# One product of block 0's second matmul gets a second level, and W2's operand sums move along the schedule

## The chip, the cores and the metric

The kernel runs on one core of a Trainium2 chip. Times are device microseconds (us) of one launch; a version's time is the median of its runs. A ratio is the mean time of one kernel's fast runs over the mean of the other's fast runs of the same rounds, so it is not quite the ratio of the medians quoted beside it. Engines are called PE (TensorE), DVE (VectorE), ACT (ScalarE), POOL (GpSimd) and SP (SyncE, which here only issues transfers). In the lines of the profile, `arena` is the kernel's on-chip memory, bX, bY, bZ and bW are the banks that PE's products go to, and `w1s` and `w2s` hold parts and sums of W1 and W2 in device memory. L432 is line 432 of the kernel; the numbers shift by some lines from version to version. The granted clock is PE's clock as a share of full speed.

## The reference

```python
# x (16, 512, 768), w1 (768, 3072), b1 (3072), w2 (3072, 768), all float32
y = np.matmul(x, w1) + b1
y = 0.5 * y * (1.0 + erf(y / np.sqrt(2.0)))
return np.matmul(y, w2)
```

## The kernel before

The 8192 rows of x form eight blocks of 1024. Both matrix products use the scheme that multiplies two matrices, each cut into 2 x 2 parts, with seven products of half size in place of eight; the price is sums of parts before ("operand sums") and after. In blocks 2 to 7 the second matmul (by W2) uses the scheme twice: each of its seven products is again seven. Blocks 0 and 1 are different, because there the operand sums of W2 have still to be made and stored for the later blocks.

- Block 0's second matmul is four **row units** (`Unit2`), each seven products of 12 matmuls of 384 columns.
- Block 1's has three products (1, 4, 2) done with a second level, one **two-level unit** each (`UnitH`, 7 x 12 matmuls of 192 columns), and then four **lean** row units with the four other products.

The order is: row units of block 0, two-level units, lean units, block 2. While PE works on a unit, "fill" functions put other work into six slots of it, in program order: DVE sums, and transfers on the SP queue. A W2 sum is popped from the list `slow`; its store to memory is put on SP one slot later, by `drain`.

```python
        def split_w2(p, t=None, q=None):                  # four operand sums of W2 for product p
            ...
            for n, a, b in ((7, b22, b12), (5, b12, b11), (6, b22, t[5]), (4, b21, t[6])):
                def f(n=n, a=a, b=b):
                    tt(t[n], a, b, SUB)                    # DVE
                    puts.append(lambda: put(n, t[n]))      # SP: stored when drain() comes next
                later(WB, f, slow if q is None else q)
            ...

        def fill_lean(sb, k, slot):                        # lean unit k of block 1
            U = NU + k
            drain(slot)
            ...                                            # row sums
            if k == 0 and slot == 6:
                for t in range(3):
                    transpose_dma(2, t)                    # x of block 2, tiles 0 to 2: SP
                load_next_x(2, range(3, 6))                # tiles 3 to 5: POOL, into the same 3 buffers
            if k == 1 and slot == 2:
                for n in range(2):
                    load_wt(2 * NH + n)                    # two W1 tiles for block 2: SP
            if k == 1 and slot == 4:
                for t in range(3, 6):
                    transpose_dma(2, t)
                load_next_x(2, range(6, 8))
            if k == 2 and slot == 4:
                for t in range(6, 8):
                    transpose_dma(2, t)
            if k == 3 and slot == 4:
                x_sums(2, soon)                            # DVE; PE wants the first at block 2's start
            ...                                            # two more W1 tiles (k == 3, slot 5)
```

So x of block 2 goes through three buffers: load, transpose, load into the freed buffer, transpose, and once more. I call this the **x chain**.

Of the kernel before, what the change touches and what calls it, by code (L numbers as in the profile page):

```python
# [22 lines left out]
def kernel(  # L23
# [129 lines left out]
    o_stage = o_wt + 2 * WT_N  # L153
# [7 lines left out]
    for slot, off in ((T2, o_x0), (T1, o_x0 + W2_N + 2 * GS_N), (T4, o_x1 + XT_N)):  # L161
        w2v[slot] = cut(off, W2_N, "p (h c n) -> p h c n", h=2, c=NH)
    GS = [cut(o, GS_N, "p (c r) -> p c r", c=NH)
          for o in (o_x0 + W2_N, o_x0 + W2_N + GS_N, o_x1, o_x1 + GS_N)]
    osbs = [cut(o, PAR).bitcast(FP32).rearrange("p (a n) -> p a n", a=2)
            for o in (o_wt, o_x1 + 2 * GS_N)]
    par1, par4 = [cut(o, PAR).bitcast(FP32).rearrange("p (r t h n) -> p r t h n", r=2, t=2, h=2)
                  for o in (o_wt, o_x1 + 2 * GS_N)]
    par11 = cut(o_w2, W2P).bitcast(FP32).rearrange("p (c n) -> p c n", c=NH)[:, 0:8, 0:N4].rearrange(
        "p (r t h) n -> p r t h n", r=2, t=2)  # L170
    osbs1 = [cut(XT_N + k * PAR, PAR).bitcast(FP32).rearrange("p (a n) -> p a n", a=2)
             for k in range(2)]

    def lev_strip(c, r):
        return [Gs[0][k // 2][:, c:c + NQ, k % 2, r:r + 2 * P] for k in range(4)]
# [10 lines left out]
    with tc.manual_schedule():  # L186
# [58 lines left out]
        staged = [0]  # L245
# [6 lines left out]
        def split_w2(p, t=None, q=None):  # L252

            b11, b12, b21, b22 = quarters(p)

            def put(q, src):
                nc.sync.dma_start(out=w2s[p, q][:], in_=src)

            if t is None:
                t = {n: stage[(staged[0] + k) % len(stage)] for k, n in enumerate((7, 5, 6, 4))}  # L260
                staged[0] += 4
            for n, a, b in ((7, b22, b12), (5, b12, b11), (6, b22, t[5]), (4, b21, t[6])):
                def f(n=n, a=a, b=b):
                    tt(t[n], a, b, SUB)
                    puts.append(lambda: put(n, t[n]))
                later(WB, f, slow if q is None else q)
            return t
# [73 lines left out]

        def half_sums(c, ks=(0, 1, 2)):
# [16 lines left out]
        def lev_sums(i, c0=0, c1=NQ, ks=(0, 1, 2, 3), q=None, p=None, levs=None):  # L359

            A = OPERAND[ORDER[i] if p is None else p]
# [50 lines left out]
        class Unit2:  # L412
# [9 lines left out]
            def mm(self, p, dst, first, c0, c1):  # L422
                if self.lean and p in (1, 2, 4):
                    return
# [3 lines left out]
                for c in range(c0, c1):  # L428
                    a = {1: G1[:, c, 0, r], 2: G2[:, c, 0, r], 4: G2[:, c, 1, r],
# [12 lines left out]
            def c12(self):  # L442
                return self.o[:, 0, N2:N]

            def c22(self):
                return self.o[:, 1, N2:N]

            def right_done(self):
                c0 = N2 if self.lean else 0
                nc.sync.dma_start(out=orr[:, self.sb * 8 + self.u, c0:N], in_=self.o[:, 0, c0:N])  # L450

            def left_done(self, row, bank):
                if self.lean and row == 0:
                    return
                if self.lean:
                    tt(self.o[:, 1, 0:N2], bank[:, 0:N2], self.rows(par4), ADD)
                else:
                    nc.scalar.copy(out=self.o[:, row, 0:N2], in_=bank[:, 0:N2])
                if row == 1:
                    nc.sync.dma_start(out=orr[:, self.sb * 8 + NU + self.u, :],  # L460
                                      in_=self.o[:, 1, :])
# [98 lines left out]
        class UnitH(Unit3):  # L560

            def __init__(self, g, sb, m):
                self.g, self.sb, self.p = g, sb, HYBRID[m]
# [3 lines left out]
                self.add = par1 if self.p == 2 else None  # L567
                self.dst = {1: par1, 4: par4, 2: par11}[self.p]
                self.alloc = lambda: None

            def mm(self, q, dst, first, c0, c1):
                A, s = OPERAND[self.p], self.lev
# [18 lines left out]

        HYBRID = (1, 4, 2)
        hyb_lev = [lev_strip(0, 0), lev_strip(NQ, 0), lev_strip(0, 2 * P)]
        hyb_w = {}

        def wb_at(off):
            return cut(off, WB, "p (c n) -> p c n", c=NQ)
# [52 lines left out]
        def p6(u):  # L650
            u.mm(6, bY[u.g % 2], False, 0, u.C)
            on_act = isinstance(u, Unit3) or (isinstance(u, Unit2) and u.lean) or (isinstance(u, Unit1) and u.sb >= ONE and u.g % 2)
# [287 lines left out]
        def fill_mm2_one(sb, U, slot):  # L940
            if slot == 1:
# [5 lines left out]
                if U == 0:  # L947
                    for p in (1, 2, 3, 5, 6, 7, 4):
                        raw_w2(p)
                    for p in (5, 6, 7, 3):  # L950
                        split_w2(p)
                    hyb_w[1] = split_w2(1)
# [8 lines left out]
            if slot == 4 and U + 1 < NU:  # L961
                g_sum(1, U + 1, q=soon)
            if U + 1 == NU and slot == 2:
                lev_sums(None, p=HYBRID[0], levs=hyb_lev[0])
# [10 lines left out]
        def fill_hyb(sb, m, slot):  # L975
            drain(slot)
            if m == 0 and slot == 1:
                o = (o_x0 + W2_N, o_x0 + W2_N + WB, o_wt + PAR, o_wt + PAR + WB)
                hyb_w[4] = split_w2(4, dict(zip((5, 6, 7, 4), map(wb_at, o))), queue)
                lev_sums(None, p=HYBRID[1], levs=hyb_lev[1])  # L980
            if m == 1 and slot == 1:
                lev_sums(None, p=HYBRID[2], levs=hyb_lev[2])
                o = (o_x1, o_x1 + WB)
                hyb_w[2] = split_w2(2, dict(zip((5, 6, 7, 4), [wb_at(k) for k in o] +
                                                [stage[staged[0] % len(stage)], hyb_w[1][7]])), queue)
            if m == 2 and slot == 2:
# [4 lines left out]
            if slot == 6:  # L991
                flush(queue)
                if m == 2:
                    load_next_x(2, range(3))

        def fill_lean(sb, k, slot):
# [10 lines left out]
            if slot == 4 and k + 1 < NU:  # L1007
                g_sum(1, U + 1, q=soon)
            if slot > 1:
                sums(1200)  # L1010
            if k == 0 and slot == 6:
# [18 lines left out]
            if slot == 6 and k == NU - 1:  # L1030
                flush(soon)
                flush(queue)
                drain(slot)
# [95 lines left out]
```

## Time and profile before

| | before |
|---|---|
| median, range | 852.62 us, 852.40 to 853.05 (6 runs) |
| span of the profiled run | 850.6 us |
| granted clock | 1.0 |
| block 0's row units to the end of the lean units, first to last 384-column matmul start | 109.76 us |
| matmul spacing, 384 and 192 columns | 162.5 and 82.5 ns |

The prediction shows the lines that carry the bound (start, length, queue, line, operation, output<-input, count): PE's pieces follow each other without a gap. Two more lines will be needed, from the timelines of SP and POOL of the kernel before (start, length, queue, line, operation, output<-input, count): the two W1 tiles, and load 6 of x.

```profile
200.23 1.01 SPq L219 DMA_DIRECT2D arena<-w1s  x2
214.10 0.54 POOL L299 DMA_DIRECT2D arena<-in_x_dram  x1 [8.65 <-DMA arena<-arena]
```

The W1 tiles are issued 3.5 us ahead of x loads 3 to 5, and have landed (205.86 and 209.13) before those land (210.2 to 212.2). In brackets is POOL's idle time and what ended it: load 6 waited for a transpose, `arena<-arena`, to free its buffer.

### The profile page before, as it was taken

What the parts mean: (1) busy time and instruction counts of PE and PEld (TensorE: products, weight loads), DVE (VectorE), ACT (ScalarE), POOL (GpSimd) and SP (SyncE); (2) the same over time, 40 slices, a digit from 0 to 9 for tenths busy, and PEclk for the clock granted to TensorE, in tenths of its full rate; (3) what the DMA queues carried; (4) which work ended last, traced back from release to release, by engine and by line L of the source; (5) the groups of instructions that cost most, each with busy time, mean ns of one, the idle gap of its engine ahead of it and who ended that gap; (6) DMA issues with size and microseconds to landing.
All of it is one profiled execution on the core that took longest, in us unless ns stands there. A gap on an engine that the chain in (4) does not pass through costs nothing.

```text
span 850.6 us, 16487 instructions
## 1 busy us (share of the span) xinstructions
PE 845.5 (99%) x6432; PEld 569.6 (67%) x6432; DVE 667.2 (78%) x1126; ACT 421.3 (50%) x686; POOL 84.1 (10%) x135
## 2 busy tenths in 40 slices
PE   9999999999999999999999999999999999999998
PEld 5444446687544897449964499645995469944798
DVE  5766678786657998679976799768996699956998
ACT  4777761122277513773148822487216771267611
POOL 5021100002100002000020000210002100010000
PEclk9999999999999999999999999999999999999999
DMA  9998777659999699987999689995999949984398
GB/s 229 199 284 170 165 160 277 234 195 218 234 331 207 194 332 372 296 177 236 332 381 266 155 291 335 361 293 111 315 351 344 283 111 328 356 311 172 101 310 283
DMA packets 143522, 219.05 MB, mean 258 GB/s; under 512 B 61756, under 2 KB 84724, under 8 KB 143444
## 3 DMA queue, kind: packets, MB, share of 16 engines
q1 hardware_dynamic: 117824, 179.74, 67.3%
q0 software_dynamic: 25440, 38.15, 20.6%
q8 instruction: 50, 0.82, 0.4%
q14 instruction: 28, 0.23, 0.1%
q10 hardware_dynamic: 180, 0.11, 0.0%
HBM read 180.30 MB, written 47.87 MB: 268 GB/s over the span
## 4 chain that ended last, share of the span: by engine, by line
PE 95%; DMA 4%; DVE 0%; ACT 0%; issue 0%; POOL 0%; DVEq 0%; ACTq 0%
PE bY L388 21%; PE bY L493 15%; PE bX L388 14%; PE bX L493 10%; PE bZ L388 7%; PE bW L388 7%; PE bZ L493 5%; PE bW L493 5%; PE bY L432 5%; DMA arena<-in_x_dram 2%; PE bZ L432 2%; PE bW L432 2%; PE bX L432 2%; DMA arena<-in_w_dram 1%; PE bY L580 1%; PE bX L580 1%
## 5 line engine op out<-in xcount | busy, mean ns | idle before, releaser
L191 DVE TENSOR_TENSOR arena<-arena 128x768 f16<-128x768 f16 (+4 forms) x630 | 403.4, 671 | 7.5 <-PE bW L432 1.1
L388 PEld LDWEIGHTS <-arena 128*128 128x128 f16 x1974 | 192.6, 98 | 224.0 <-issue 0.4
L493 PEld LDWEIGHTS <-arena 128*128 128x128 f16 x3528 | 292.1, 98 | 8.4 <-issue 0.4
L388 PE MATMUL bY<-arena 128*128 128x512 f16 x846 | 214.4, 379 | 0.1
L613 DVE TENSOR_TENSOR arena<-bY,arena 128x512 f32<-128x512 f32 (+1 forms) x102 | 69.4, 681 | 127.0 <-PE bY L388 90.3
L493 PE MATMUL bY<-arena 128*128 128x192 f16 x1500 | 138.3, 246 | 0.0
L388 PE MATMUL bX<-arena 128*128 128x512 f16 x564 | 138.2, 379 | 0.0
L606 ACT COPY bY<-bX 128x512 f32<-128x512 f32 (+1 forms) x143 | 78.6, 550 | 119.4 <-DVE arena L542 82.0
L404 ACT ACTIVATE arena<-arena,b1t 128x1024 f16<-128x1024 f32 x94 | 108.0, 1149 | 54.0 <-DVE arena L641 54.0
L626 ACT COPY arena<-bW 128x512 f32<-128x512 f32 (+1 forms) x147 | 81.1, 552 | 90.7 <-PE bW L493 43.9
L493 PE MATMUL bX<-arena 128*128 128x192 f16 x1020 | 93.1, 246 | 0.1
L641 DVE TENSOR_TENSOR arena<-bZ,arena 128x512 f32<-128x512 f32 (+1 forms) x102 | 69.3, 679 | 22.2 <-PE bZ L388 18.2
L388 PE MATMUL bW<-arena 128*128 128x512 f16 x282 | 76.2, 379 | 0.0
L388 PE MATMUL bZ<-arena 128*128 128x512 f16 x282 | 76.2, 379 | 0.0
L432 PEld LDWEIGHTS <-arena 128*128 128x128 f16 x528 | 51.6, 98 | 34.1 <-issue 0.2
L525 POOL DMA_DIRECT2D out_dram<-arena x42 | 30.6, 729 | 406.4 <-DVE arena L637 370.2
L409 ACT ACTIVATE arena<-bX,b1t 128x512 f16<-128x512 f32 x94 | 64.0, 681 | 10.0 <-PE bX L388 10.0
L409 ACT ACTIVATE arena<-bY,b1t 128x512 f16<-128x512 f32 x94 | 63.4, 674 | 0.0
L657 ACT COPY bZ<-bY 128x512 f32<-128x512 f32 (+1 forms) x54 | 29.0, 537 | 65.7 <-DVE arena L641 31.4
L299 POOL DMA_DIRECT2D arena<-in_x_dram x60 | 32.7, 550 | 248.2 <-DMA arena<-arena 137.9
L493 PE MATMUL bW<-arena 128*128 128x192 f16 x504 | 48.4, 246 | 0.0
L493 PE MATMUL bZ<-arena 128*128 128x192 f16 x504 | 48.4, 246 | 0.0
(60 smaller groups left out, 401.8 us busy)
## 6 DMA issues: line engine op xcount, KB each, us to landing
arena<-w2s SPq DMA_DIRECT2D x294, 288.0 KB, 4.7
arena<-w1s SPq DMA_DIRECT2D x72, 672.0 KB, 7.0
out_dram<-arena POOLq DMA_DIRECT2D x42, 384.0 KB, 7.2
w2s<-arena SPq DMA_DIRECT2D x49, 288.0 KB, 3.8
arena<-in_x_dram POOLq DMA_DIRECT2D x60, 192.0 KB, 7.1
w1s<-arena SPq DMA_DIRECT2D x12, 672.0 KB, 6.1
arena<-in_w_dram POOLq DMA_DIRECT2D x17, 384.0 KB, 7.6
out_dram<-arena SPq DMA_DIRECT2D x17, 384.0 KB, 3.4
```

What stands on the lines that cost most here:

```text
L191: nc.vector.tensor_tensor(out=o, in0=a, in1=b, op=op)
L299: nc.gpsimd.dma_start(out=xhs[t], in_=xr[:, sb * 8 + t, :])
L388: nc.tensor.matmul(out=dst[:, 0:RH], lhsT=w1_op(self.wt, slot)[:, c, :], rhs=a[:, c, :], start=first and c == 0, stop=c == self.C - 1, ski ...
L404: nc.scalar.activation(out=self.G[1][:, hi, :, :], in_=self.tmp, func=GELU, bias=b1t[:, 2 * hi + 1:2 * hi + 2])
L409: nc.scalar.activation(out=self.G[0][:, hi, row, :], in_=bank[:, 0:RH], func=GELU, bias=b1t[:, 2 * hi:2 * hi + 1])
L432: nc.tensor.matmul(out=dst[:, 0:N2], lhsT=a, rhs=w[:, :, c, :], start=first and c == 0, stop=c == self.C - 1, skip_group_check=True)
L493: nc.tensor.matmul(out=dst[:, t * N4:(t + 1) * N4], lhsT=a, rhs=w[:, c, :], start=first and c == 0 and t == ts[0], stop=c == NQ - 1, skip_ ...
L525: eng.dma_start(out=orr[:, s0:s0 + 2, right * N2:(right + 1) * N2], in_=self.dst[:, r].rearrange("p t h n -> p t (h n)"))
L606: nc.scalar.copy(out=bY[u.g % 2][:, 0:u.F], in_=bX[u.g % 2][:, 0:u.F])
L613: nc.vector.tensor_tensor(out=u.c22(), in0=bY[u.g % 2][:, 0:u.F], in1=w[:, 0:u.F], op=ADD)
L626: nc.scalar.copy(out=w[:, 0:u.F], in_=bW[:, 0:u.F])
L641: nc.vector.tensor_tensor(out=u.c12(), in0=bZ[:, 0:u.F], in1=w[:, 0:u.F], op=ADD)
```

## The change

Its intent: product 2 of block 0 leaves the four row units and becomes a fourth two-level unit, seven eighths of the columns. Its operands need DVE time and buffers in block 0's units, so only W2 products 6, 1, 4 and 2 are summed there; 7 and 5 move into the two-level units and 3 into the lean units. The core of the diff (buffer addresses and names cut):

```diff
             def mm(self, p, dst, first, c0, c1):          # Unit2
-                if self.lean and p in (1, 2, 4):
+                if p == 2 or self.lean and p in (1, 4):
                     return
...
-        HYBRID = (1, 4, 2)
+        HYBRID = ((0, 2), (1, 1), (1, 4), (1, 2))
...
         def fill_mm2_one(sb, U, slot):                    # block 0's row units
-                    for p in (5, 6, 7, 3):
-                        split_w2(p)
-                    hyb_w[1] = split_w2(1)
+                    for p, t in ((6, (0, 1, 2, 3)), (1, (4, 5, 0, 1)), (4, (2, 3, 4, 5)), (2, (0, 1, 2, 5))):
+                        split_w2(p, t)
...
         def fill_hyb(sb, m, slot):                        # two-level units
+            if m == 1 and slot == 6:
+                split_w2(7, (6, 7, 6, 7))
+                split_w2(5, (6, 7, 6, 7))
+            if slow and (m == 1 or slot in (1, 4, 6)):
+                slow.pop(0)[1]()
...
         def fill_lean(sb, k, slot):
+            if k == 0 and slot == 4:
+                split_w2(3, (1, 2, 3, 4))
             if slot > 1:
                 sums(1200)
+            if slow and slot in (2, 5):
+                slow.pop(0)[1]()
```

Also new: six stored W2 quarters of products 1 and 4 are read back (`load_w2s`), copies of one bank go from DVE to ACT, and the output buffers are laid out anew.

More of the change, by code (lines that the diff above doesn't have):

```diff
@@ L152 @@
     tmps1 = [tmp_at(o_tmp + 4 * k * RH) for k in range(2)]
-    o_stage = o_wt + 2 * WT_N
+    o_stage = o_wt + 2 * N + PAR
     stage = [cut(o_stage + k * WB, WB, "p (c n) -> p c n", c=NQ)
@@ L164, with strip, wb_at @@
           for o in (o_x0 + W2_N, o_x0 + W2_N + GS_N, o_x1, o_x1 + GS_N)]
-    osbs = [cut(o, PAR).bitcast(FP32).rearrange("p (a n) -> p a n", a=2)
-            for o in (o_wt, o_x1 + 2 * GS_N)]
-    par1, par4 = [cut(o, PAR).bitcast(FP32).rearrange("p (r t h n) -> p r t h n", r=2, t=2, h=2)
-                  for o in (o_wt, o_x1 + 2 * GS_N)]
+    osbs = [[cut(o, n).bitcast(FP32) for o, n in zip(oo, (2 * N2, 2 * N))]
+            for oo in ((o_x1 + 2 * GS_N + 2 * N + 2 * N2, o_wt),
+                       (o_x1 + 2 * GS_N + 2 * N, o_x1 + 2 * GS_N))]
+    assert 2 * N + 4 * N2 <= PAR
+    par02, par1, par4 = [cut(o, PAR).bitcast(FP32).rearrange(
+        "p (r t h n) -> p r t h n", r=2, t=2, h=2) for o in (o_wt + 2 * N, 2 * XT_N, o_x1 + 2 * GS_N)]
     par11 = cut(o_w2, W2P).bitcast(FP32).rearrange("p (c n) -> p c n", c=NH)[:, 0:8, 0:N4].rearrange(
         "p (r t h) n -> p r t h n", r=2, t=2)
-    osbs1 = [cut(XT_N + k * PAR, PAR).bitcast(FP32).rearrange("p (a n) -> p a n", a=2)
-             for k in range(2)]
-    def lev_strip(c, r):
-        return [Gs[0][k // 2][:, c:c + NQ, k % 2, r:r + 2 * P] for k in range(4)]
+    osbs1 = [[cut(XT_N + k * PAR, 2 * N2).bitcast(FP32),
+              cut(XT_N + k * PAR + 2 * N2, 2 * N).bitcast(FP32)] for k in range(2)]
+    def strip(h, a, c, r):
+        return Gs[0][h][:, c:c + NQ, a, r:r + 2 * P]
+    def wb_at(off):
+        return cut(off, WB, "p (c n) -> p c n", c=NQ)
+    hyb_lev = [[strip(0, 0, 0, 0), strip(1, 1, 0, 0), Gs[0][1][:, 0:NQ, 0, 2 * P:RH], strip(1, 1, NQ, 0)],
+               [strip(0, 1, 0, 0), strip(0, 0, NQ, 0), strip(0, 1, NQ, 0), strip(0, 0, 0, 2 * P)],
+               [strip(0, 1, 0, 2 * P), strip(0, 0, NQ, 2 * P), strip(0, 1, NQ, 2 * P),
+                strip(1, 1, NQ, 2 * P)],
+               [strip(0, 0, 0, 0), strip(0, 1, 0, 0), strip(0, 0, NQ, 0), strip(0, 1, NQ, 0)]]
+    spare = stage + [wb_at(2 * XT_N + PAR + k * WB) for k in range(2)]
+    hyb_w = {2: {7: stage[0], 5: stage[1], 6: stage[2], 4: stage[5]},
+             1: dict(zip((7, 4, 5, 6), map(wb_at, (o_x0 + W2_N, o_x0 + W2_N + WB, o_x1, o_x1 + WB)))),
+             4: {7: wb_at(o_x1), 4: wb_at(o_x1 + WB), 5: stage[3], 6: stage[4]}}
     b1t = wp.tile([P, 2 * NH], FP32, name="b1t")
@@ L244 @@
         SLOT = {1: B11, 2: B21, 3: B22, 4: T4, 5: T1, 6: T2, 7: T3}
-        staged = [0]
         puts, raws = [], []
@@ L250, in quarters, with split_w2 @@
             return w[:, 0, 0:NQ, :], w[:, 1, 0:NQ, :], w[:, 0, NQ:NH, :], w[:, 1, NQ:NH, :]
-        def split_w2(p, t=None, q=None):
+        def split_w2(p, t, q=None):
             b11, b12, b21, b22 = quarters(p)
@@ L257, in put @@
                 nc.sync.dma_start(out=w2s[p, q][:], in_=src)
-            if t is None:
-                t = {n: stage[(staged[0] + k) % len(stage)] for k, n in enumerate((7, 5, 6, 4))}
-                staged[0] += 4
+            t = {n: spare[k] for n, k in zip((7, 5, 6, 4), t)}
             for n, a, b in ((7, b22, b12), (5, b12, b11), (6, b22, t[5]), (4, b21, t[6])):
@@ L266, in split_w2, with load_w2s @@
                 later(WB, f, slow if q is None else q)
-            return t
+        def load_w2s(p, qs):
+            for q in qs:
+                nc.sync.dma_start(out=hyb_w[p][q], in_=w2s[p, q][:])
         def raw_w2(p):
@@ L340, with operand @@
                    5: GA, 6: GB, 7: G1[:, :, 1, :]}
+        HYBRID = ((0, 2), (1, 1), (1, 4), (1, 2))
+        def operand(sb, p):
+            return OPERAND[p] if sb else Gs[0][1][:, :, 0, :]
         def half_sums(c, ks=(0, 1, 2)):
@@ L357, in lev_of, with lev_sums @@
             return lev[(i - 1) % 2] if i else lev0
-        def lev_sums(i, c0=0, c1=NQ, ks=(0, 1, 2, 3), q=None, p=None, levs=None):
-            A = OPERAND[ORDER[i] if p is None else p]
+        def lev_sums(i, c0=0, c1=NQ, ks=(0, 1, 2, 3), q=None, m=None):
+            A = OPERAND[ORDER[i]] if m is None else operand(*HYBRID[m])
+            levs = None if m is None else hyb_lev[m]
             a11, a12 = A[:, c0:c1, 0:2 * P], A[:, NQ + c0:NQ + c1, 0:2 * P]
@@ L428, in mm @@
                 for c in range(c0, c1):
-                    a = {1: G1[:, c, 0, r], 2: G2[:, c, 0, r], 4: G2[:, c, 1, r],
+                    a = {1: G1[:, c, 0, r], 4: G2[:, c, 1, r],
                          3: GS[3][:, c, :], 5: GS[0][:, c, :], 6: GS[1][:, c, :],
@@ L442, in c12 @@
             def c12(self):
-                return self.o[:, 0, N2:N]
+                return self.o[0]
             def c22(self):
-                return self.o[:, 1, N2:N]
+                return self.o[1][:, N2:N]
             def right_done(self):
-                c0 = N2 if self.lean else 0
-                nc.sync.dma_start(out=orr[:, self.sb * 8 + self.u, c0:N], in_=self.o[:, 0, c0:N])
+                nc.sync.dma_start(out=orr[:, self.sb * 8 + self.u, N2:N], in_=self.o[0])
             def left_done(self, row, bank):
-                if self.lean and row == 0:
+                if row == 0:
+                    if not self.lean:
+                        nc.scalar.copy(out=self.rows(par02), in_=bank[:, 0:N2])
                     return
                 if self.lean:
-                    tt(self.o[:, 1, 0:N2], bank[:, 0:N2], self.rows(par4), ADD)
+                    tt(self.o[1][:, 0:N2], bank[:, 0:N2], self.rows(par4), ADD)
                 else:
-                    nc.scalar.copy(out=self.o[:, row, 0:N2], in_=bank[:, 0:N2])
-                if row == 1:
-                    nc.sync.dma_start(out=orr[:, self.sb * 8 + NU + self.u, :],
-                                      in_=self.o[:, 1, :])
+                    nc.scalar.copy(out=self.o[1][:, 0:N2], in_=bank[:, 0:N2])
+                nc.sync.dma_start(out=orr[:, self.sb * 8 + NU + self.u, :], in_=self.o[1])
         units3 = {}
@@ L562, in __init__ @@
             def __init__(self, g, sb, m):
-                self.g, self.sb, self.p = g, sb, HYBRID[m]
+                self.g, (self.sb, self.p) = g, HYBRID[m]
                 self.lev, self.w = hyb_lev[m], dict(hyb_w[self.p])
@@ L566, in __init__ @@
                 self.w.update({1: b11, 2: b21, 3: b22})
-                self.add = par1 if self.p == 2 else None
-                self.dst = {1: par1, 4: par4, 2: par11}[self.p]
+                self.add = {0: par02, 1: par1}[self.sb] if self.p == 2 else None
+                self.dst = {1: par1, 4: par4, 2: par11}[self.p] if self.sb else par02
                 self.alloc = lambda: None
             def mm(self, q, dst, first, c0, c1):
-                A, s = OPERAND[self.p], self.lev
+                A, s = operand(self.sb, self.p), self.lev
                 for c in range(NQ):
@@ L590, in finish @@
                             in_=self.dst[:, n // 2, n % 2])
-        HYBRID = (1, 4, 2)
-        hyb_lev = [lev_strip(0, 0), lev_strip(NQ, 0), lev_strip(0, 2 * P)]
-        hyb_w = {}
-        def wb_at(off):
-            return cut(off, WB, "p (c n) -> p c n", c=NQ)
         def p1(u, c0, c1):
@@ L651, in p6 @@
             u.mm(6, bY[u.g % 2], False, 0, u.C)
-            on_act = isinstance(u, Unit3) or (isinstance(u, Unit2) and u.lean) or (isinstance(u, Unit1) and u.sb >= ONE and u.g % 2)
+            on_act = isinstance(u, Unit3) or isinstance(u, Unit2) or (isinstance(u, Unit1) and u.sb >= ONE and u.g % 2)
             if isinstance(u, Unit3) and u.add is not None:
@@ L962, in fill_mm2_one @@
                 g_sum(1, U + 1, q=soon)
+            if U + 2 == NU and slot == 5:
+                lev_sums(None, m=0, ks=(0, 1, 3))
+            if U + 1 == NU and slot == 4:
+                lev_sums(None, m=0, ks=(2,))
             if U + 1 == NU and slot == 2:
-                lev_sums(None, p=HYBRID[0], levs=hyb_lev[0])
+                lev_sums(None, m=1, ks=(0, 1, 2))
             if slot > 1:
@@ L977, in fill_hyb @@
             if m == 0 and slot == 1:
-                o = (o_x0 + W2_N, o_x0 + W2_N + WB, o_wt + PAR, o_wt + PAR + WB)
-                hyb_w[4] = split_w2(4, dict(zip((5, 6, 7, 4), map(wb_at, o))), queue)
-                lev_sums(None, p=HYBRID[1], levs=hyb_lev[1])
-            if m == 1 and slot == 1:
-                lev_sums(None, p=HYBRID[2], levs=hyb_lev[2])
-                o = (o_x1, o_x1 + WB)
-                hyb_w[2] = split_w2(2, dict(zip((5, 6, 7, 4), [wb_at(k) for k in o] +
-                                                [stage[staged[0] % len(stage)], hyb_w[1][7]])), queue)
-            if m == 2 and slot == 2:
+                load_w2s(1, (7, 4))
+                lev_sums(None, m=1, ks=(3,))
+            if m == 0 and slot == 4:
+                load_w2s(1, (5, 6))
+            if m == 0 and slot == 5:
+                lev_sums(None, m=2)
+            if m == 1 and slot == 5:
+                lev_sums(None, m=3, ks=(0, 1, 2))
+            if m == 1 and slot == 6:
[3 more added lines that the diff above has]
+                slow.pop(0)[1]()
+            if m == 2 and slot == 1:
+                load_w2s(4, (7, 4))
+                lev_sums(None, m=3, ks=(3,))
+            if m == 3 and slot == 2:
                 for k in (0, 1):
@@ L992, in fill_hyb @@
                 flush(queue)
-                if m == 2:
+                if m == 3:
                     load_next_x(2, range(3))
@@ L1032, in fill_lean @@
                 flush(queue)
+                flush(slow)
                 drain(slot)
```

## The prediction

> **What bounds the kernel now.** I read the page first, then the chain of work in order of time for 116 to 236 us (the stretch that the change touches), then the engines one by one there. The page's busy line and the shares of the chain:
>
> ```profile
> PE 845.5 (99%) x6432; PEld 569.6 (67%) x6432; DVE 667.2 (78%) x1126; ACT 421.3 (50%) x686; POOL 84.1 (10%) x135
> PE 95%; DMA 4%; DVE 0%; ACT 0%; issue 0%; POOL 0%; DVEq 0%; ACTq 0%
> ```
>
> TensorE (PE) is busy 99% and is 95% of the chain; the 4% of DMA is the head, before the first product. Busy matmul time alone can hide gaps, so I looked at the spacing of pieces in the chain, at the hand-over from block 0's units (L432, 384 columns) to the two-level units (L580, 192 columns) and back:
>
> ```profile
> 168.91 1.95 PE bX L432 x12
> 170.86 0.99 PE bX L580 x12
> 171.85 1.95 PE bY L432 x12
> ...
> 193.54 0.99 PE bX L580 x12
> 194.53 1.02 PE bY L580 x12
> 195.56 1.95 PE bW L432 x12
> ```
>
> Each piece starts where the last ended (168.91 + 1.95 = 170.86). Twelve matmuls of 384 columns take 1.95 us, 162.5 ns each; twelve of 192 take 0.99, 82.5 ns each. The only irregular pieces between 119 and 236 us are one of 1.02 (0.03 too long) and one of 2.01 (0.06 too long). Taking every matmul's start to the next start, the excess over these paces sums to some 4.5 us in the whole kernel, 3.6 of it in the first 40 us. So **PE's columns set the time**, and no wait is left to remove in the changed stretch: it can gain only what it takes off PE, and lose whatever stall it makes.
>
> **What the Trainium skill says.** "TensorE: Matmul & The Clock Gate", section "Wait — 56ns, not 53.3ns?": warm start-to-start is columns / 2.4 GHz plus about 2.5 ns. That is 162.5 and 82.5 ns for 384 and 192; the trace agrees to the digit, and granted clock is 1.00 in every 10 us stretch after the head. So splitting a matmul in two costs only 2.5 ns. "Perfetto Trace Analysis", "Identifying the Most-Contended Engine": matmul busy share is no measure of headroom, look at weight loads; PEld is at 67% here, up to 10.00 of 10 us in the two-level stretches, where the spacing still is 82.5, so weight loads hide. "DMA: Bandwidth & Descriptors", "Anatomy of one DMA — SWDGE (gpsimd) path": a DMA's semaphore wait happens on the issuing sequencer, so one waiting store holds all behind it on that queue. The trace agrees: SP sat 13.1 us on four output stores between 192 and 245 us. Same page, "Issuing engines are not separate DMA queues": all queues share the 16 engines and interleave; here a 192 KB load of x took 4.7 us with little beside it and 7.3 us among stores.
>
> **The change, part by part.**
> *Removed from PE:* product 2 of block 0's four row units: 4 x 12 = 48 matmuls of 384 columns, 48 x 162.5 = 7.80 us.
> *Added to PE:* one two-level unit, 7 products x 6 chunks x 2 row tiles = 84 matmuls of 192 columns, 84 x 82.5 = 6.93 us. (That is seven eighths of the columns, plus 36 x 2.5 ns.) Both lie on the path. **Net -0.87 us**, the whole possible gain: 0.1%.
> *VectorE (DVE):* four operand sums of 1536 (950 ns each, 3.8 us) and six PSUM adds of 384 (about 0.55 each, 3.3 us) are new; four copies of bY to bZ (560 ns) go to ACT. W2 sums are 28 in both kernels (752 ns each), but block 0's units hold 16 instead of 20 (-3.0 us); eight now start in the second two-level unit of block 1's stage and run through its units, four more in the lean units. The tightest row unit is the third: six W2 sums 4.5, four row sums 3.8, two lev sums 1.9, two evictions 1.1, together 11.3 of its 11.7 us. Before, a 13.65 us unit carried about 10. Tight, but operands are made most of a unit (8 us or more) ahead, so I expect no stall.
> *ACT:* six copies of about 470 ns more; ACT is busy 1 to 4 of 10 us there. Beside.
> *DMA:* six 288 KB reloads of W2 operands, which have landed in about 2 to 5 us in this stretch; the closest is wanted 5.9 us after the eviction that precedes it. Hidden, with 1 us or so to spare. The 28 W2 stores are as many as before, but twelve move late: about six go into the lean units' time on the SP queue.
>
> **The place where I expect trouble** is the lean stage, where x of block 2 is loaded and transposed through only three buffers. These lines are from the timelines of POOL, SP and DVE:
>
> ```profile
> 203.78 1.67 POOL L299 DMA_DIRECT2D arena<-in_x_dram  x3
> 195.22 4.91 SPq L305 DMA_TRANSPOSE arena<-arena  x3
> 210.25 3.88 SPq L305 DMA_TRANSPOSE arena<-arena  x3
> 218.85 3.23 SPq L305 DMA_TRANSPOSE arena<-arena  x2
> 224.73 3.68 DVE L191 TENSOR_TENSOR arena<-arena 128x1536 f16<-128x1536 f16 x4
> 227.50 0.65 PE bW L388 x3
> ```
>
> Read as a chain: transposes 0 to 2 issue at 195.2 to 200.1 and free the buffers; loads 3 to 5 go at 203.78 and land at 210.2 to 212.2; transposes 3 to 5; loads 6 and 7 at 214.10 and 215.10, landing at 218.8 and 220.9; transposes 6 and 7, the last landed at 223.62. At 224.73 DVE forms the x sums, and at 227.50 PE wants the first. That sum takes 0.95 us, so the last transpose may land until about 226.5: **2.9 us of slack**.
>
> Let T = 201.44, where PE ends the last two-level unit's product 4. Before, transposes 0 to 2 had been issued by T - 1.3, because nothing on SP ahead of them waited for DVE. After, a W2 store stands ahead of them; its sum is ninth in the list and comes on DVE after the eviction that follows T. Eviction to T + 0.5, sum to T + 1.25, store issued, first transpose at about T + 1.9, then 1.3 us apart. They land near T + 5.6, 6.5, 7.8 (3 to 3.75 us as the second three did), where the loads of 3 to 5 left at T + 2.3 to 3.5 before. With the old latencies: loads land T + 12.2 to 14.8, transposes 3 to 5 T + 16 to 17.7, loads 6 and 7 issue T + 16.1 and 16.9, land T + 20.8 and 22.7, last transpose lands at T + 25.5, that is 226.9: 0.4 us past the slack. Six stores of 288 KB on the same DMA engines, and DVE being a little late in the last two-level unit (evictions, sums and reused W2 staging buffers take nearly all of its 6.93 us), make it somewhat more. I estimate a new stall of 0 to 1.5 us at block 2's first unit, 0.6 in the middle.
>
> Sum: 852.58 - 0.87 + 0.5 = **852.2 us**.
>
> **The rivals.** (a) Everything hides: the full 0.87 is kept, 851.7. For it: the before-trace absorbs all its DVE and DMA work without a stall in this stretch, and early loads may finish faster when less is in flight. Against: the slack of 2.9 us against a shift of over 3. (b) The x chain slips further: each of its stages meets a W2 store, or DVE holds a store for some us more, and block 2 starts 2 to 3 us late, 853.5 to 854.5. For: SP works in order, and DMA is busy nearly all of 200 to 225 us. Against: the late W2 stores are spread over three units. (c) DVE becomes the bound in block 0's third unit (11.3 of 11.7 us by names) and PE waits for row sums: up to 1 us. Against: before, DVE ran 9.42 of 10 us at 130 to 140 with no stall, and the next unit has only about 9 us of work. (d) A reload of a W2 operand lands late and PE waits up to 1 us in the two-level units. Against: a worked slack of about 1 us.
>
> **Range and chances.** The best possible is 851.7, less about 0.4 for scatter between runs (852.4 to 853.05 before); the bad end is rival (b). Eight in ten: 851.2 to 853.9. I give rival (a) some 40%, a stall under 1.5 us 45%, more 15%. Two per cent is 17 us; nothing here is of that size either way, so within 2% is 0.98, and slower and faster get 0.01 each.
>
> **What would show each step.** In the changed profile: 480 matmuls of 384 columns and 336 of 192 in these stages instead of 528 and 252; four row units of block 0 1.95 us shorter each; a two-level stage longer by 6.93; spacing still 162.5 and 82.5 ns. The chain shows whether stretched pieces appear: at the first L388 pieces of block 2 after the lean units (my step), in the row units (rival c), or at L580 pieces (rival d). On SP, the first three transposes should follow a W2 store and come some 6 us later, counted from the end of the last two-level unit. If they come early, my stall falls. If block 2 starts with no stretched piece, the time should be 851.7. The prediction is wrong upward if a reload or a staging buffer makes PE wait where I counted slack, and downward only if the kernel before had stalls that the chain doesn't show.

## The result, and the profile after

| | before | after |
|---|---|---|
| median (6 runs each) | 852.62 us | 857.65 us |
| range | 852.40 to 853.05 | 857.48 to 858.82 |
| ratio of fast runs | | 1.0062, 95% interval 1.0049 to 1.0075 |
| row units to lean units, first to last 384-column start | 109.76 us | 114.92 us |
| granted clock of the profiled run | 1.0 | 0.998 |

The kernel is 5.0 us slower, where 852.2 was predicted with 853.9 as the upper end. The stretch from row units to lean units is 5.16 us longer, so all of it is there; from its end to the last matmul the kernel is as long as it was (616.95 and 616.74 us). The page of the changed kernel, its busy line and its chain:

```profile
PE 846.4 (99%) x6468; PEld 572.0 (67%) x6468; DVE 671.5 (78%) x1132; ACT 423.1 (49%) x692; POOL 85.5 (10%) x139
PE 93%; DMA 4%; DVE 1%; issue 1%; SPq 0%; ACT 0%; POOLq 0%; DVEq 0%
```

PE has 36 matmuls more, as planned (84 added, 48 removed), and is still "99% busy": the loss is not visible in this line. The chain's shares tell more: PE has fallen from 95% to 93%, and SP's queue has appeared in it. PE's timeline at the change from the lean units to block 2 (L453 and L409 are L432 and L388 of the kernel before):

```profile
224.09 0.81 PE L409 MATMUL bX<-arena 128*128 128x512 f16 x3
228.73 3.75 PE L453 MATMUL bY<-arena 128*128 128x384 f16 x12 [3.83 <-ACT bZ L670]
232.78 0.81 PE L409 MATMUL bW<-arena 128*128 128x512 f16 x3 [0.30 <-DVE arena L206]
```

PE stands still for 3.83 us, then twelve matmuls that should take 1.95 us take 3.75, and then there is a second short wait. Against the known paces, matmul starts are 3.99 us late at the first gap, 1.64 us more over the next twelve (up to 158 ns on each, 320 in place of 162.5: half clock, and the profile's granted clock is 0.50 there) and 0.47 at the second gap. That is 6.10 us, and 6.10 - 0.87 = 5.2 us, the measured loss. Ahead of them, the row units and two-level units run without a gap over 0.04 us, at the old paces.

Who made PE wait? The trace names ACT, behind it DVE, behind it an output store (waits of PE and of DVE: total us, times, longest):

```profile
PE bY L453 <- ACT bZ L670: 3.8, 1, 3.8
DVE arena L626 <- DMA out_dram<-arena: 7.7, 1, 7.7
```

But the chain that ended last, followed back from the first product of block 2 that waited (`PE bW L409`), takes another way (start, length, what; short pieces left out):

```profile
201.93 0.68 DVE arena L206
...
202.62 0.32 SPq L271
...
203.05 4.78 DMA arena<-arena
...
208.43 7.90 DMA arena<-in_x_dram
...
216.35 4.23 DMA arena<-arena
...
221.10 4.84 DMA arena<-in_x_dram
...
225.96 3.85 DMA arena<-arena
229.81 1.96 issue
231.77 0.97 DVE arena L206
...
232.78 0.81 PE bW L409 x3
```

Read from the top: a W2 sum on DVE, its store on SP (L271), a transpose of x, a load of x, a transpose, a load, the last transposes, the x sum, PE. This is the x chain, headed by a W2 sum that the change put there. (The 1.96 us called issue are covered by the last transpose: it was issued at 228.96, when the last x load had landed, and landed at 231.69, 0.08 us before the x sum.) Without gaps PE would have wanted the x sum at 224.09 + 0.65 + 1.95 = 226.69 us; it got it at 232.78, 6.09 us later. So the wait that the trace names at the first gap and the slow matmuls after it seem to lie in the shadow of the x chain. SP's timeline shows the queue's order:

```profile
195.59 7.35 SPq L271 DMA_DIRECT2D w2s<-arena  x3
203.05 4.78 SPq L320 DMA_TRANSPOSE arena<-arena  x3
207.92 1.00 SPq L234 DMA_DIRECT2D arena<-w1s  x2
216.35 4.75 SPq L320 DMA_TRANSPOSE arena<-arena  x3
```

Three W2 stores stand first, the last waiting for DVE until 202.62; the transposes follow at 203.05 (195.22 before) and the W1 tiles at 207.92 (200.23 before). Now the W1 tiles go out together with x loads 3 to 5 (208.43 to 209.96), and those take 7.90, 8.77 and 9.87 us to land, where they took 6.46, 6.87 and 7.26.

### The profile page after: what moved, and what is told of

The parts are those of the page before. It is cut to its first block, busy times and chain, and to the rows that moved or that the text cites. A ratio compares the mean times of both kernels' runs of the same rounds, so it can differ in the third digit from the quotient of the medians.

```text
span 856.0 us, 16592 instructions
## 1 busy us (share of the span) xinstructions
PE 846.4 (99%) x6468; PEld 572.0 (67%) x6468; DVE 671.5 (78%) x1132; ACT 423.1 (49%) x692; POOL 85.5 (10%) x139
## 4 chain that ended last, share of the span: by engine, by line
PE 93%; DMA 4%; DVE 1%; issue 1%; SPq 0%; ACT 0%; POOLq 0%; DVEq 0%
PE bY L409 21%; PE bY L513 15%; PE bX L409 14%; PE bX L513 10%; PE bW L409 7%; PE bZ L409 7%; PE bZ L513 5%; PE bW L513 5%; PE bY L453 3%; DMA arena<-in_x_dram 2%; DMA arena<-arena 2%; PE bZ L453 1%; PE bY L600 1%; PE bX L453 1%; PE bW L453 1%; PE bX L600 1%
## 5 line engine op out<-in xcount | busy, mean ns | idle before, releaser
L206 DVE TENSOR_TENSOR arena<-arena 128x1536 f16<-128x1536 f16 (+6 forms) x634 | 406.7, 672 | 9.0 <-issue 2.3
L409 PEld LDWEIGHTS <-arena 128*128 128x128 f16 x1974 | 192.4, 98 | 224.6 <-issue 0.7
L409 PE MATMUL bY<-arena 128*128 128x512 f16 x846 | 214.5, 379 | 0.0
L409 PE MATMUL bX<-arena 128*128 128x512 f16 x564 | 138.2, 379 | 0.0
L654 DVE TENSOR_TENSOR arena<-bZ,arena 128x512 f32<-128x512 f32 (+1 forms) x102 | 69.3, 679 | 20.2 <-PE bZ L409 18.2
L409 PE MATMUL bW<-arena 128*128 128x512 f16 x282 | 76.2, 379 | 0.3 <-DVE arena L206 0.3
L409 PE MATMUL bZ<-arena 128*128 128x512 f16 x282 | 76.2, 379 | 0.0
L453 PEld LDWEIGHTS <-arena 128*128 128x128 f16 x480 | 47.3, 99 | 36.0 <-DVE arena L206 3.3
L670 ACT COPY bZ<-bY 128x512 f32<-128x512 f32 (+1 forms) x58 | 30.8, 532 | 79.3 <-DVE arena L654 37.4
```

Source lines behind the costliest of these rows:

```text
L206: nc.vector.tensor_tensor(out=o, in0=a, in1=b, op=op)
L409: nc.tensor.matmul(out=dst[:, 0:RH], lhsT=w1_op(self.wt, slot)[:, c, :], rhs=a[:, c, :], start=first and c == 0, stop=c == self.C - 1, ski ...
L453: nc.tensor.matmul(out=dst[:, 0:N2], lhsT=a, rhs=w[:, :, c, :], start=first and c == 0, stop=c == self.C - 1, skip_group_check=True)
L654: nc.vector.tensor_tensor(out=u.c12(), in0=bZ[:, 0:u.F], in1=w[:, 0:u.F], op=ADD)
L670: nc.scalar.copy(out=bZ[:, 0:u.F], in_=bY[u.g % 2][:, 0:u.F])
```

## The experiments

The theories. **A, order:** the SP queue works in order, so W2 stores that wait for DVE hold back the transposes and W1 tiles. **B, traffic:** the moved stores' bytes crowd the DMA engines, wherever they stand. **C, output store:** the wait that the trace names at the first gap is the cause. **D, the unit:** the added two-level unit itself costs time.

### 1. Transposes ahead of three W2 stores (A against B and D)

```diff
@@ fill_lean
+            if k == 0 and slot == 1:
+                for t in range(3):
+                    transpose_dma(2, t)
             drain(slot)
...
             if k == 0 and slot == 6:
-                for t in range(3):
-                    transpose_dma(2, t)
                 load_next_x(2, range(3, 6))
```

> The changed kernel with one thing moved: x's transposes 0 to 2 of block 2 stand ahead of the last three W2 stores on the SP queue; work and traffic are the same. Theory A (the order on SP: the transposes wait behind a store whose sum DVE makes after the last two-level unit): they issue near 195.3 to 199 us as in the kernel before, the x chain gets its 2.9 us of slack back, no stall, 851.8 us (851.4 to 852.3). Theory B (the late stores and reloads crowd the DMA engines): the traffic is the same, so 856 to 858. Theory D (the added two-level unit itself costs time): 857.6.

Measured: correct, 855.69 us (855.03 to 857.42), ratio 1.0041 (1.0027 to 1.0055). Its SP timeline:

```profile
194.85 5.67 SPq L320 DMA_TRANSPOSE arena<-arena  x3
200.61 2.24 SPq L271 DMA_DIRECT2D w2s<-arena  x3
205.21 1.30 SPq L234 DMA_DIRECT2D arena<-w1s  x2
```

The transposes are as early as in the kernel before, and the gap at block 2's x sum shrinks from 6.09 to 2.63 us. That is order, with the same work and bytes. But the miss is as large as the hit: 851.8 was expected. The W1 tiles, at 205.21, are still 5 us late, behind the stores, and x loads 3 to 5 land at 209.06, 212.49 and 215.10 (210.24, 211.22 and 212.15 before). Transposes 3 to 5, next on SP behind the W1 tiles, land 8.35, 6.90 and 4.96 us after issue (2.98 and 2.82 for the last two before). The profile is of the fastest of the five runs; the two slowest have a granted clock of 0.999 and 0.997 instead of 1.0.

### 2. Transposes ahead of the last W2 store only

```diff
+            if k == 0 and slot == 6:
+                for t in range(3):
+                    transpose_dma(2, t)
             drain(slot)
```

(and the old place removed, as in the first run)

> The changed kernel with transposes 0 to 2 moved ahead of the one W2 store that they share a slot with, so behind the store issued at 199.09 and no longer behind that of 202.62. Theory A: transposes start at about 199.5 instead of 203.05, 3.6 us sooner; the 6.1 us by which block 2's first sum was late shrinks to 2 to 3, so 853.5 to 855.0 us. Theory B: 856 to 858.

Measured: correct, 855.24 us, four runs in two groups: 854.14 and 854.17 at a granted clock of 1.0, 856.30 and 856.97 at 0.998. The gap in the profile is 2.82 us, as expected; the time lies just over the expected range because of the second group. PE's timeline in a run of that group:

```profile
229.97 1.44 PE L409 MATMUL bW<-arena 128*128 128x512 f16 x3 [2.66 <-DVE arena L206]
231.21 2.89 PE L453 MATMUL bZ<-arena 128*128 128x384 f16 x12
```

After the wait the next matmuls are slow again. They start 320 ns apart for 384 columns, which is half clock (granted clock 0.50 from 229.4 to 232.7 us). So a gap of this size can cost 2 us beyond itself (the last section compares this with the Trainium skill).

### 3. The output store on another queue (C against A)

```diff
-                nc.sync.dma_start(out=orr[:, self.sb * 8 + NU + self.u, :], in_=self.o[1])
+                (nc.scalar if self.lean else nc.sync).dma_start(out=orr[:, self.sb * 8 + NU + self.u, :], in_=self.o[1])
```

> The changed kernel with the lean units' bottom-row output stores issued from ACT's queue, so that the store of lean unit 0 no longer stands behind transposes 3 to 5. Theory C (the wait that the trace names at PE's 3.99 us gap: ACT's copy of bY waits for DVE, which waited 7.75 us for that output store): the gap goes and the time falls to about 852 us. Theory A: that gap lies in the shadow of the x chain; DVE no longer waits for the store, but block 2's first x sum still comes at about 232 us, PE has one gap of some 6 us instead of several, and the time stays at 857 to 859.5 us.

Measured: correct, 860.93 us. The first gap is gone, and the waits of PE hold one line:

```profile
PE bW L409 <- DVE arena L206: 7.1, 1, 7.1
```

So C is refuted: without the named wait, PE waits for the x sum alone, longer. The time is above the range that A gave, by 1.4 us: the x sum came 1.4 us later still (x loads 3 to 5 took 8.41 to 11.10 us, now beside an output store issued at 210.94), and fifteen slow matmuls now come after the chain's end instead of in its shadow.

### 4. The kernel before with four late sums and nothing else (A against D)

```diff
@@ the kernel before
-                    for p in (5, 6, 7, 3):
+                    for p in (5, 6, 7):
@@ fill_lean
+            if k == 0 and slot == 1:
+                split_w2(3)
             if slot > 1:
                 sums(1200)
+            if slow and slot in (2, 5):
+                slow.pop(0)[1]()
```

(and what is left is flushed at the end of the lean units)

> The kernel before with one part of the change alone: product 3's four W2 sums moved from block 0's units into the lean units, two of them ahead of transposes 0 to 2; no added two-level unit. Theory A: the transposes start about T + 2 instead of T - 6 and block 2 starts 3 to 6 us late, 855.5 to 859 us. Theory D (the added unit is the cause): 852.6 us, as before. Theory B: only four stores of 288 KB moved, under 1 us.

Measured: correct, 860.04 us, ratio 1.0087: this part alone loses more than the whole change. The transposes start at the same late time:

```profile
203.57 5.15 SPq L305 DMA_TRANSPOSE arena<-arena  x3
```

PE has a gap of 5.53 us at the x sum and half-clock matmuls after it. The size is above the expected range; the clock was not in the expectation.

### 5. No moved sums at all (A and B against D)

The changed kernel without the twelve moved sums and stores; later blocks read a stored quarter in their place. Its output is wrong, which doesn't matter for the time.

```diff
-                split_w2(7, (6, 7, 6, 7))
-                split_w2(5, (6, 7, 6, 7))
...
-                split_w2(3, (1, 2, 3, 4))
```

> Wrong result on purpose: the changed kernel without the twelve W2 sums and stores that the change moved out of block 0's units (products 7, 5 and 3; later blocks read a stored quarter in their place, the same bytes). The added two-level unit stays. If the moved sums are the whole cause (theory A, by order, traffic or both), nothing stands ahead of transposes 0 to 2 and of the W1 loads: 851.3 to 852.2 us, the 0.87 us that the prediction worked out. Theory D (the added unit itself costs): still 854 or more.

Measured: 852.27 us (852.05 to 852.52), 852.79 for the kernel before in the same rounds, ratio 0.9994 (0.9980 to 1.0007). No gap; the stretch from row units to lean units is 108.89 us, 0.87 under the kernel before. **In its stretch the added unit gains what was worked out**, and D is refuted. The median is 0.5 lower, not 0.87, and just outside the expected range: in this run's profile the part before the row units was 0.52 us longer (over all profiles it varies by 0.8) and the part behind the lean units 0.45.

### 6. Late stores with almost no bytes (A against B)

```diff
+                if p in (3, 5, 7):
+                    nc.sync.dma_start(out=w2s[p, q][:, 0:1, 0:16], in_=src[:, 0:1, 0:16])
+                    return
                 nc.sync.dma_start(out=w2s[p, q][:], in_=src)
```

> Wrong result on purpose: the changed kernel with those twelve stores cut to 16 columns of 1152, so that they hold the SP queue and wait for DVE as they did but move almost no bytes. If the queue's order is the cause, transposes 0 to 2 still start at about 203 us and the W1 loads at 208: 855.5 to 857.7 us. If the stores' bytes crowd the DMA engines (theory B): 852 to 853.5 us.

Measured: wrong, 856.06 us. The transposes still start at 202.49 and the W1 tiles at 206.94. With hardly a byte moved, 3.3 of the 5 us loss stay: order. In time the bytes are worth some 1.8 us, but in the x chain they are worth more: the x sum is 2.89 us late instead of 6.09. The half-clock matmuls that follow, 1.40 us, come after the chain here and not in its shadow, so they hide part of that. So of these 6.09 us order alone makes about half; the other half comes with the bytes, in that order.

### 7. Transposes and W1 tiles first; W1 tiles alone first

Both need the W1 tiles' place free, so the sums of 7 and 5 were staged elsewhere, in four buffers. The move of the transposes is that of the first run; the W1 loads' and the staging's:

```diff
-                split_w2(7, (6, 7, 6, 7))
-                split_w2(5, (6, 7, 6, 7))
+                split_w2(7, (0, 1, 2, 5))
+                split_w2(5, (0, 1, 2, 5))
...
+            if k == 0 and slot == 1:
+                for n in range(2):
+                    load_wt(2 * NH + n)
             drain(slot)
```

> The changed kernel with transposes 0 to 2 and after them the two W1 loads ahead of the last three W2 stores (the late sums of products 7 and 5 stage in four free buffers so that the W1 tiles' place is free). The first run showed the transposes on time and loads 3 to 5 of x still landing 1.3 to 3 us late, beside W1 loads that now came at 205.2 instead of 200.2. If that collision, itself made by the order on SP, is the rest of the cause: x loads 3 to 5 land by about 212, no stall over 0.5 us, 851.7 to 852.8 us, level with or under the kernel before. If the late stores' own traffic is the rest: 854 to 856 us as in the first run.

> The changed kernel with the W1 loads alone moved ahead (and the same staging buffers as in the run with both), the transposes left behind the stores. The transposes start at 203 to 204 us as in the changed kernel, but x loads 3 to 5 no longer share the DMA engines with two W1 tiles: they take 6.5 to 7.5 us instead of 7.9 to 9.9, the x chain is 1.5 to 3 us shorter, 854 to 856.3 us. If W1's place is of no account: 857.6.

Measured: both 852.77 us and 857.33 us, and **both wrong by mistake**: from the code, the staging overwrote W2 quarters that the last two-level unit reads again. Work and traffic are the same kind and amount, so I read the times with that in mind. With both moved, the time is in the expected range: the gap at the x sum is gone; one of 1.06 us came at 211.43 us, where DVE waited 2.5 us for a store before reusing a staging buffer. With W1 alone moved, x loads 3 to 5 took 4.8 to 5.5 us, not 7.9 to 9.9, and the gap at the x sum became 3.08 us plus half-clock matmuls; but the time hardly fell (854 to 856.3 was expected), since the slow matmuls moved out of the chain's shadow.

### 8. The same, mended

Four other staging buffers (6, 8, 6, 8 and 9, 10, 6, 8, three of them new, in a part of memory that is free by then), transposes and W1 tiles first (and their old places removed):

```diff
@@ fill_hyb
-                split_w2(7, (6, 7, 6, 7))
-                split_w2(5, (6, 7, 6, 7))
+                split_w2(7, (6, 8, 6, 8))
+                split_w2(5, (9, 10, 6, 8))
@@ fill_lean
+            if k == 0 and slot == 1:
+                for t in range(3):
+                    transpose_dma(2, t)
+                for n in range(2):
+                    load_wt(2 * NH + n)
             drain(slot)
```

> The changed kernel with transposes 0 to 2 and the two W1 loads ahead of the last three W2 stores, as in the earlier run with both, but with correct staging (that run overwrote W2 quarters that the last two-level unit still needed; its one gap of 1.06 us was DVE waiting 2.5 us for a store before it reused a staging buffer). Correct results. If the order on SP and the collision with W1 that it made are the whole cause: no gap over 0.5 us, 851.8 to 852.5 us, 0.3 to 1.0 under the kernel before. If the late stores' traffic still costs: 853 to 854.

Measured: correct, 853.39 us (852.78 to 854.12), 852.86 before, ratio 1.0008 (0.9995 to 1.0022). Of the changed kernel's 5 us, 4.5 are back. One gap is left, 0.49 us at the x sum: x loads 3 to 5 land at 210.4 to 213.9 beside three W2 stores. The time lies in the range expected if the late stores' traffic still costs, so order is not quite the whole cause.

The second version also has no W2 sum in lean unit 0 (`if slow and slot in (2, 5) and k > 0`):

> The same, and no W2 sum in lean unit 0, so that no store of product 3 shares the DMA engines with x loads 3 to 5. If the traffic beside those loads still costs in the run above, this one is 0.5 to 1 us faster than it; if nothing is left to gain, both are equal within 0.3 us at 851.8 to 852.5.

Measured: correct, 853.48 us: equal to the first, but both above the expected range. The x sum is on time, and the loss has moved: a gap of 1.0 us at 236.2, where PE waits for a W1 tile that SP issued at 227.88 behind the last W2 stores.

### 9. Two more buffers for x (a miss)

Loads 6 and 7 get their own buffers and are issued with 3 to 5: on top of the mended kernel, and alone on top of the changed one.

```diff
@@ xh_of, the place of x tile t of block sb
+            if sb == 2 and t >= 6:
+                return cut(o_wt + 2 * N + (2 * WB if t == 6 else 0), K)
...
-                load_next_x(2, range(3, 6))
+                load_next_x(2, range(3, 8))
```

> The mended kernel (transposes 0 to 2 and the W1 loads ahead of the stores) with two more buffers for x of block 2, in a place that is free by then: loads 6 and 7 no longer wait for transposes 3 and 4 and are issued near 205 instead of 216 to 218. If the x chain's lack of slack is all that is left (0.49 us of gap in the profile, 0.5 us of median over the kernel before): last transpose lands by 222 to 224, no gap at block 2, 851.8 to 852.4 us, under both kernels. If the added unit has a cost elsewhere: 853 or more.

> The changed kernel with those two buffers alone, order on SP untouched. The chain is one round of load and transpose shorter, about 6 to 8 us, but its start stays 8 us late: block 2's first sum comes at about 226 instead of 232.7 against a need at 226.7, so a gap of 0 to 1.5 us, 852.0 to 854.0 us. If the chain through the three buffers were not the cause, 857.6.

Measured: both correct, 858.14 (855.03 to 861.46) and 860.52 us, far from the expectation. In the first, loads 6 and 7 landed early, at 217.0 and 218.4, but POOL, no longer held by those two, then issued the loads of *block 3* sooner, as SP issued transposes 6 and 7 (POOL, then SP):

```profile
219.61 0.53 POOL L317 DMA_DIRECT2D arena<-in_x_dram  x1 [12.88 <-DMA arena<-arena]
```

```profile
221.20 3.94 SPq L323 DMA_TRANSPOSE arena<-arena  x2
```

Those two transposes landed 7.8 and 7.2 us after issue (2.9 and 2.7 in the kernel before). Nor did SP come to them sooner than in the mended kernel (221.25), though load 6 had landed 4.2 us earlier: the queue's order again, with two late W2 stores (219.00 and 219.48) and an output store (220.71) ahead of them. The three buffers had also been a brake on the loads of the block after. That the collision and the place on SP are the cause is read from the trace; no run removed either alone.

### 10. W1's last two tiles earlier as well

Both mended versions with W1 tiles 26 and 27 issued right behind transposes 6 and 7 (`k == 2 and slot == 5` for `k == 3 and slot == 5`).

> The mended kernel without a W2 sum in lean unit 0 (its profile: no gap at block 2's first sum, one of 1.0 us at 236.2, a W1 tile issued at 227.88 behind the last W2 stores and landed late), with the W1 tiles 26 and 27 issued right behind transposes 6 and 7 instead. If place in the SP order is all that is left and the added unit is free: no gap over 0.3 us, 851.9 to 852.5 us, 0.3 to 0.9 under the kernel before. If the late stores' bytes have a price wherever they stand: 852.8 to 854.

> The first mended kernel (W2 sums in lean unit 0 kept, median 853.39, a gap of 0.49 us at block 2's first sum from x loads 3 to 5 that share the DMA engines with three W2 stores), with those W1 tiles early too. The x chain is not helped, so the gap of 0.3 to 1 us stays: 852.6 to 853.6. Only if the bytes beside x loads 3 to 5 are not what costs is it as fast as the run above.

Measured: the first is correct, 852.62 us (852.19 to 853.08) to 852.73 before, ratio 0.9998 (0.9986 to 1.0011). Its SP timeline and its chain at the start of block 2:

```profile
195.11 4.68 SPq L321 DMA_TRANSPOSE arena<-arena  x3
199.84 1.06 SPq L235 DMA_DIRECT2D arena<-w1s  x2
```

```profile
224.45 0.65 PE bX L410 x3
225.09 2.01 PE bY L454 x12
227.11 0.65 PE bW L410 x3
```

No gap (the time is 0.1 us above the expected range): the stretch is 108.89 us, the full 0.87 under the kernel before, with every late store still made. The second stays at 853.57 with a gap of 1.01 us at the x sum. So the late bytes have no price of their own in the stretch; what costs is standing beside x loads 3 to 5. In the median little of the 0.87 shows, 0.1 us and within noise: in the profiled run the part ahead of the row units took 0.48 us longer and the part behind the lean units 0.24. Over the runs of these rounds the median span of the core is 0.5 us shorter (850.5 to 851.0); why some 0.4 of that is lost outside the span is open. No version clearly beats the kernel before.

## Why the prediction was wrong

**Right: the bound, the gain and the place.** Outside the half-clock stretch PE kept its paces of 162.5 and 82.5 ns, has 36 matmuls more, and the stretch without stalls is 0.87 us shorter (runs without the late sums, and the last one). The x chain was named as the place of the loss, for the reason given: the transposes stand behind a W2 store. Rivals (c) and (d) did not come: no gap in row units or two-level units.

**Wrong: one term of the sum, "a new stall of 0 to 1.5 us at block 2's first unit, 0.6 in the middle".** It measured 6.09 us. T is where PE ends the last two-level unit's product 4; after the change T = 201.44 - 0.87 + 0.29 (the row units started 0.29 us later) = 200.86.

| step of the x chain, us after T | predicted | measured |
|---|---|---|
| transposes 0 to 2 issued | first 1.9, then 1.3 apart | 2.2, 3.7, 5.7 |
| landed | 5.6, 6.5, 7.8 | 7.0, 7.7, 8.6 |
| x loads 3 to 5 landed | 12.2 to 14.8 | 15.5, 17.1, 19.0 |
| x loads 6 and 7 issued | 16.1, 16.9 | 20.2, 21.9 |
| last transpose landed | 25.5 | 30.8 |

The step that failed is **"With the old latencies"**. The start was nearly right: the first transpose left at T + 2.2, not 1.9. Then I left everything else where it was, but the two W1 tiles, which my working never lists, stand on the same queue behind the same stores; they moved too, from 3.5 us ahead of x loads 3 to 5 to the same moment as those loads. The loads took up to 9.87 us. The runs bear this out: with transposes on time and W1 late, a gap of 2.63 us is left; with both on time, none to 1.01 us (runs 7, 8 and 10), by which stores stand beside the loads. I had even read the W1 tiles' effect in the kernel before without naming it: the load of 7.3 us "among stores" (204.89 to 212.15) had both tiles beside it, until 205.86 and 209.13.

The other part of the same step is the late stores' bytes, for which I allowed "somewhat more". With them nearly gone and the order as it was, the last transpose landed at T + 27.7 and not 30.8. So of the 5.3 us that the chain ran over my 25.5, the bytes account for 3.1. The two parts do not simply add: what both lengthen are the same x loads and transposes.

Two slips change little: the sum takes a stall of 0.5 where the text has 0.6, and the first transpose coming "some 6 us later" is 8.1 by the working itself (8.4 measured).

**Missing: the clock.** A PE gap of some 3 us or more was followed by half-clock matmuls, 1.64 us here. In the changed kernel itself this lay in the chain's shadow and added nothing; in the second and third run it did.

**Missing: a second wait behind the same queue.** An output store stuck behind transposes 3 to 5 held DVE 7.7 us and made PE's first gap. The third run shows that it cost nothing, being covered by the x chain.

The range's upper end, 853.9, came from rival (b), "2 to 3 us late", which was the right rival with the wrong size and with a chance of 15%.

## What to carry to other kernels

When a transfer that waits for a late producer is put on an in-order queue, every transfer behind it moves, not just the one under study: list them all, and work out which of them then meet. A wait that the trace names at a gap need not be the cause; follow the chain that ended last, and take the named wait away in a run. And count a gap of about 3 us on PE at more than its length: here 2.66 us of idle time brought half clock, 2.46 us did not.

## What the Trainium skill lacked or had wrong

- "TensorE: Matmul & The Clock Gate", "What's actually happening", gives an idle window of about 3.4 us, free-running, as what drops the clock to half. Here matmuls went to half clock (320 ns for 384 columns, as the page implies) after starts that were 2.8 and 2.9 us late, 2.66 and 2.73 us of it idle time (the second run, and the run with small stores); after 2.63 us (2.46 idle), in the first run's profile, they did not. Two of the second run's four executions were some 2 us slower at a granted clock of 0.998 and two were not, at 1.0, at equal code.
- "DMA: Bandwidth & Descriptors" has the shared engines and the waits at the issuing sequencer, but no figure for a transpose's landing beside other transfers. Here a transpose between buffers landed 2.7 to 2.9 us after issue in the kernel before (DMA share 0.64 to 0.84 in the profile's view of these stretches), 7.8 us beside loads of x (1.15), and 8.35 us when issued 3.9 us after the first of two W1 tiles (1.08). Nor has it one for a load's landing in company: 192 KB loads of x issued together with two 672 KB W1 tiles took 7.90 to 9.87 us (5.84 to 7.71 with the late W2 stores cut to almost no bytes), with those tiles ahead by 3.5 us 6.46 to 7.26, and with them ahead by 14 us 4.8 to 5.5.
